# Where the sums for T4 and the low parts of T3 are made: in the last blocks of gMLP, or inside the first pair's products

## The chip, the cores and the metric

The kernel runs on one core of a Trainium2 chip. The metric is the device time of one execution in microseconds (us). Of the kernel before there are three timed runs and one profiled execution. The engines are named as the profile names them: PE is TensorE's matmuls, PEld its weight loads, DVE is VectorE, ACT is ScalarE, POOL is GpSimd, and SP is SyncE, which issues transfers.

## The reference, cut to what matters

One decoder layer over 1,024 tokens of width 1,024: a normalised input xn goes through one large projection `w_in`, its parts through three mixers (gMLP, RG-LRU, SSD), and the mixers' outputs are merged under gates and followed by an MLP.

```python
hn = rms_norm(h, norm_mix_g[l])
proj = jnp.einsum('bsd,de->bse', hn, w_in[l])
za, zb, zc, xbc, dt_raw, g_raw = jnp.split(proj, SPLIT_POINTS, axis=-1)
ya = gmlp_mixer(za, ...)
yb = rg_lru_mixer(zb, ...)
yc = ssd_mixer(zc, xbc, dt_raw, ...)
gates = jax.nn.sigmoid(g_raw.reshape(bsz, seq, N_BRANCHES, D_MODEL) + b_gate[l])
```

The change concerns only how the operands are made for the last part of `proj`: the gate columns `g_raw` (three branches), the SSD gate `zc` and part of the LRU gate.

## The kernel before, in words

**Split operands.** Every float32 operand of a matmul is kept as two fp32r tiles, a high part (a cast on ACT, line 132) and a low part (the difference, on DVE, line 133). `split` makes both. A product of two operands is three matmuls: high by high, high by low, low by high.

**Plain units.** The first part of `proj` is computed in units of 128 columns (`unit_in`, `one_unit`, lines 558 and 571): 48 matmuls of 128x512 at line 555 into a PSUM tile `ps` of 128x1,024, from a pool of two. The last eight units are those of gMLP, `gmlp_unit(g)` for g = 0 to 7. Each makes a gelu of its `ps` by four steps in a row, `gelu2` (lines 235 to 238: ACT, DVE, ACT, DVE; L238 is the last read of `ps`). Its `stages` then multiply the normalised v by the mixing weights (L836 on PE, L837 on DVE) and the gelu by that on POOL (L839), and POOL issues the store (L840).

**Steps.** Generators given to `later()` are advanced by `step()`, one piece at each call; `one_unit` calls it once after each unit. `x_forms`, the operand forms of X, is queued by the stages of g = 0. The order in these units is the scheduler's, by program order and readiness.

**Pairs.** The remaining columns are made in pairs of 2 x 128 columns with seven products instead of eight, each over half the depth: `seventh`, 12 matmuls of 128x512 at line 478. X is cut into quarters B11, B12, B21, B22, the weights into A11 to A22, and sums of quarters are used: T1, T2, T3, T4 of X, S1 to S4 of the weights. T3 is B22 - B12, T2 is B11 + T3, T1 is B22 - T2, and T4 is B21 - T2. The products of one pair are, in this order, p1 = A11 B11, p2 = A12 B21, p5 = S1 T1, p6 = S2 T2, p3 = S4 B22, p7 = S3 T3, and p4 = A22 T4. p1, p6, p7 and p4 accumulate in one PSUM bank of the pool `gps`, and between them the bank is read: after p1 by L981 and after p6 by L998 on ACT, after p7 by L1006 on DVE. p2's bank is read by L986 on DVE, the bank of p5 and p3 by L992 on ACT and L1002 on DVE. p4 stands behind p1 and p2 of the next pair. `gps` takes the banks in which `ps` lay.

**The order among the pairs** is that of the code, `tc.manual_schedule()` (line 1279): between the products stand the steps that prepare the next pair's weights (cast1; sums1, which is L502 and L503; sums2, L506 and L507; cast12; cast22) and this pair's S3 and S4 (cast34), and a `step()`, and each engine takes its instructions in that order. An instruction that waits holds all that is behind it on its engine.

**T3's low part and T4 in x_forms.** For each of two tiles kp the generator makes T3 unsplit (`third`, lines 871 to 873), T2 and its split, T1 and its split, and T4 (lines 883, 884 and a split into two tiles of the pool `act`, 15 buffers). At the very end, after the units, T3 is split over the tiles of B12, which nothing needs any more.

Of the kernel before, what the change touches and what calls it, by code (L numbers as in the profile page):

```python
# [8 lines left out]
F32 = mybir.dt.float32  # L9
# [27 lines left out]
def trunk_kernel(ctx: ExitStack, tc: tile.TileContext, x, norm_mix_g, w_in, b_gate, gmlp_ln_g, gmlp_ln_b,  # L37
# [30 lines left out]
    def nm(s):  # L68
        uid[0] += 1
        return f"{s}_{uid[0]}"  # L70

    def act(shape=(P, T), dt=F32):
        return pools[0].tile(list(shape), dt, tag="act", name=nm("a"))

    def half_(shape=(P, HF), dt=F32):
        return halfp.tile(list(shape), dt, tag="half", name=nm("h"))
# [51 lines left out]
    def split(dst_hi, dst_lo, src, eng=None, cast=None):  # L128
        if cast:
            cast.tensor_copy(out=dst_hi, in_=src)  # L130
        else:
            actv(dst_hi, src, AF.Copy)  # L132
        (eng or nc.vector).tensor_tensor(out=dst_lo, in0=src, in1=dst_hi.bitcast(F32), op=ALU.subtract)  # L133
# [62 lines left out]
    X = Pairs(lambda shape, dt_: xp.tile(list(shape), dt_, tag="xn", name=nm("xn")))  # L196
# [334 lines left out]
    queue, ready, pending = [], [], []  # L531
# [4 lines left out]
    def later(gen):  # L536
        pending.append(gen)

    def step():
        for g_ in list(pending):  # L540
            try:
                next(g_)
            except StopIteration:
                pending.remove(g_)
# [279 lines left out]
    def gmlp_unit(g):  # L824
        def stages(u2):
            if g == 0:
                later(x_forms())
            elif g == 5:
                later(first_pair())
            yield  # L830
            vg = v_of.pop(g)
            y = act()
            for half in range(2):
                ps = aux()
                for i in range(4):
                    mm(ps[:, i * P:(i + 1) * P], vg[:, half * 4 + i, :], wT[:, g, :], start=True, stop=True)  # L836
                stt(out=y[:, hsl(half)].rearrange("p (c t) -> p c t", t=P), in0=ps.rearrange("p (c t) -> p c t", t=P),  # L837
                    scalar=vh[:, LNG + g:LNG + g + 1], in1=bs[:, g, :].unsqueeze(1).to_broadcast([P, 4, P]), op0=ALU.mult, op1=ALU.add)
            nc.gpsimd.tensor_tensor(out=y, in0=y, in1=u2, op=ALU.mult)  # L839
            nc.gpsimd.dma_start(out=yd["a"][g], in_=y)  # L840

        def post(ps):
            u2 = act()
            gelu2(u2, ps, T)
            later(stages(u2))
            v_group(g + 1)

        unit_in(C_U + g * P, post)
# [2 lines left out]
    XF = {n: [[X.rhs(part, 4 * kh + kk, th) for kk in range(4)] for part in range(2)]  # L851
          for n, kh, th in (("B11", 0, 0), ("B21", 1, 0), ("B22", 1, 1), ("T3", 0, 1))}

    def x_forms():
        third = []
        for n in ("T1", "T2", "T4"):
            XF[n] = [[None] * 4, [None] * 4]
        for kp in range(2):
            def quarter(part, kh, th):
                return X.tile(part, th, 2 * kh + kp).bitcast(F32)  # L860

            def in_halves(name, t):
                for kk in range(2):
                    pr = half_((P, 4, P), F32R), half_((P, 4, P), F32R)
                    for part in range(2):
                        XF[name][part][2 * kp + kk] = pr[part]
                    split(pr[0], pr[1], t[:, kk])

            third.append(act((P, 2, 4, P)))
            t3, d, e = third[kp], act((P, 2, 4, P)), act((P, 2, 4, P))  # L870
            tt(out=t3, in0=quarter(0, 1, 1), in1=quarter(0, 0, 1), op=sub)
            tt(out=e, in0=quarter(1, 1, 1), in1=quarter(1, 0, 1), op=sub)
            tt(out=t3, in0=t3, in1=e, op=ALU.add)
            yield
            tt(out=d, in0=quarter(0, 0, 0), in1=t3, op=ALU.add)
            tt(out=d, in0=quarter(1, 0, 0), in1=d, op=ALU.add)
            in_halves("T2", d)
            yield
            tt(out=e, in0=quarter(0, 1, 1), in1=d, op=sub)
            tt(out=e, in0=quarter(1, 1, 1), in1=e, op=ALU.add)  # L880
            in_halves("T1", e)
            yield
            tt(out=d, in0=quarter(0, 1, 0), in1=d, op=sub)
            tt(out=d, in0=quarter(1, 1, 0), in1=d, op=ALU.add)
            pr = act((P, 2, 4, P), F32R), act((P, 2, 4, P), F32R)
            split(pr[0], pr[1], d)
            for part in range(2):
                for kk in range(2):
                    XF["T4"][part][2 * kp + kk] = pr[part][:, kk]
            yield  # L890
        assert not queue
        for kp in range(2):
            split(X.tile(0, 1, kp), X.tile(1, 1, kp), third[kp])

    actx_pool = []
    two = (P, 2, HF)
# [194 lines left out]
    def w_load(b, name, new, key=None):  # L1091
        L[b, key or name] = [new(two) for _ in range(2)]
        for h, t in enumerate(L[b, key or name]):
            nc.sync.dma_start(out=t, in_=w_view(b, name, h))
# [7 lines left out]
    def y_first(b, new):  # L1102
        R[b, "first"] = [new(two, F32R) for _ in range(2)]
        for h, t in enumerate(R[b, "first"]):
            nc.sync.dma_start(out=t.bitcast(F32), in_=y_view(b, "B21", h))
# [10 lines left out]
    def sums_load(b):  # L1116
        w_load(b, "A21", w4, "S")
        for h in range(2):
            add_into(L[b, "S"][h], w_view(b, "A22", h))
# [10 lines left out]
    def make(b, i, s):  # L1130

        side, h = (s // 2) ^ (i == 3), s % 2
        new = op_new(b, i, side)
        pr = OP.setdefault((b, i), ([], []))[side]
        if side == 0:
            src = L[b, ("A12", "A11", "S", "A12", "S", "A21", "A22")[i]][h]
            hi, lo = new(two, F32R), new(two, F32R)
            split(hi, lo, src)
            if i == 2:
                actv(src, src, AF.Copy, scale=-1.0)  # L1140
                add_into(src, L[b, "A11"][h])
                for k in range(2 * h):
                    add_into(L[b, "A12"][k], L[b, "S"][k])
            elif i == 4:
                t = L[b, "A21"][h]
                tt(out=t, in0=L[b, "A11"][h], in1=t, op=sub)
        elif i == 0:
            lo = R[b, "first"][h]
            hi = new(two, F32R)
            split(hi, lo, lo.bitcast(F32))  # L1150
        else:
            hi, lo = new(two, F32R), new(two, F32R)
            split(hi, lo, R[b, ("", "B11", "B11", "B22", "B11", "B12", "B21")[i]][h])
            r = lambda name: R[b, name][h]
            if i == 1:
                tt(out=r("B11"), in0=r("B12"), in1=r("B11"), op=sub)
            elif i == 3:
                tt(out=r("B11"), in0=r("B11"), in1=r("B22"), op=sub)
                tt(out=r("B12"), in0=r("B22"), in1=r("B12"), op=sub)
            elif i == 4:  # L1160
                tt(out=r("B21"), in0=r("B21"), in1=r("B11"), op=ALU.add)
        pr.append((hi, lo))
# [113 lines left out]
    gx = ExitStack()  # L1276
    actx_pool.append(gx.enter_context(tc.tile_pool(name="actx", bufs=4, reuse_waits="tile")))
    z, prev = cur.pop(), None
    with tc.manual_schedule():
        z.w.cast22()  # L1280
        while z:
            nxt = Pair(*pairs.pop(0)) if pairs else None
            z.p1()
            z.w.cast34()
            step()
            z.p2()
            if prev:
                step()
                prev.p4()
            if nxt:  # L1290
                nxt.w.cast1()
            else:
                w_load(0, "A12", r4)
                y_first(0, act)
                w_load(0, "A11", w4)
            step()
            z.p5()
            if nxt:
                nxt.w.sums1()
            else:  # L1300
                make(0, 0, 2)
            step()
            z.p6()
            if nxt:
                nxt.w.sums2()
                nxt.w.cast12()
            else:
                sums_load(0)
                make(0, 0, 3)
            step()  # L1310
            z.p3()
            if nxt:
                nxt.w.cast22()
            else:
                make(0, 0, 0)
            step()
            z.p7()
            if not nxt:
                make(0, 0, 1)
            step()  # L1320
            prev, z = z, nxt
# [532 lines left out]
```

## Time and profile before

| | |
|---|---|
| timed runs | 1976.08 us median of 3 (1975.45 to 1978.53) |
| profiled execution | 1979.05 us, span of the instructions 1977.3 us |
| granted TensorE clock, mean over the span | 0.986 |
| busy: PE, DVE, ACT, POOL | 1914.5, 1409.4, 1015.5, 256.9 us |
| the last gMLP products to p4 of the first pair | 600 to 648 us from the span's start |

Busy times are sums over instructions. A row of a timeline gives the start in us from the span's start, the duration, the engine, the line, the operation, the tiles out<-in and the number of instructions taken together; in brackets stands the idle time of that engine before it, and which instruction ended that. DVE and ACT begin an instruction a little before the one in front ends, so what an instruction takes in a queue is read from one start to the next.

### The profile page before, as it was taken

The page shows a single profiled execution, that of the slowest core. Times are in us where ns is not written, and L with a number is a line of the kernel's source. Part 1 is how long each engine was busy: PE and PEld are TensorE (multiplying, and loading weights), DVE is VectorE, ACT ScalarE, POOL GpSimd, SP SyncE. Part 2 cuts the span into 40 slices and gives each one's busy share as a digit, 9 for nine tenths or more (in the row PEclk, how much of TensorE's full clock was granted, in tenths as well). Part 3 has the DMA queues.
Part 4 walks back from the last instruction along what each step waited for, and adds up shares of the span by engine and source line. Part 5 has one row for each costly group of instructions (what it writes and reads, how often), then busy time and mean ns, then how long its engine had stood idle before and what let it go on. Part 6 is the DMA issues. An engine that isn't in the chain of part 4 may idle for free.

```text
span 1977.3 us, 23724 instructions
## 1 busy us (share of the span) xinstructions
PE 1914.5 (97%) x8928; PEld 1592.9 (81%) x8928; DVE 1409.4 (71%) x2018; ACT 1015.5 (51%) x1471; POOL 256.9 (13%) x358
## 2 busy tenths in 40 slices
PE   8999999999999999999999999998999999999996
PEld 7998878787887787878778888776788887888885
DVE  5485868686768676767767888347666657788787
ACT  6425858586633545454554544167555555243243
POOL 4111121112233010101010110000211110000000
PEclk8999999999999999999999999999999999999998
DMA  4246574666664252535298987321544458554632
GB/s 158 60 142 138 119 146 112 141 129 138 154 161 128 83 173 87 169 91 165 98 296 277 253 230 191 138 104 60 193 136 165 134 181 303 171 162 117 190 115 88
DMA packets 211015, 301.25 MB, mean 152 GB/s; under 512 B 13028, under 2 KB 125876, under 8 KB 210900
## 3 DMA queue, kind: packets, MB, share of 16 engines
q1 hardware_dynamic: 167348, 158.54, 26.4%
q0 software_dynamic: 34544, 119.69, 22.7%
q10 hardware_dynamic: 9008, 21.51, 3.1%
q8 instruction: 70, 1.15, 0.3%
q14 instruction: 45, 0.37, 0.1%
HBM read 195.75 MB, written 74.58 MB: 137 GB/s over the span
## 4 chain that ended last, share of the span: by engine, by line
PE 68%; DVE 11%; issue 7%; ACT 7%; DMA 6%; POOL 1%; ACTq 0%; POOLq 0%; DVEq 0%; SPq 0%
PE aux L478 39%; PE ps L555 10%; PE gps L478 8%; PE aux L257 5%; PE aux L1376 2%; DMA a<-acs_d 2%; DVE a L578 1%; DMA raw<-in_w_in_dram 1%; DMA c<-yc_d 1%; ACT a L1425 1%; DMA wl<-raw 1%; PE aux L789 1%; DVE a L133 1%; DVE rsq_q L111 1%; DVE wt L133 1%
## 5 line engine op out<-in xcount | busy, mean ns | idle before, releaser
L555 PE MATMUL ps<-xn,wh 128*128 128x512 f32 x1088 | 294.8, 392 | 0.0
L478 PE MATMUL aux<-b,b 128*128 128x512 f32 x1152 | 264.4, 389 | 0.9 <-DVE b L133 0.9
L478 PEld LDWEIGHTS aux<-b,b 128*128 128x128 f32 x1152 | 216.1, 188 | 46.9 <-DVE b L133 1.7
L555 PEld LDWEIGHTS ps<-xn,wh 128*128 128x128 f32 x1088 | 202.9, 188 | 42.1 <-issue 0.7
L478 PE MATMUL aux<-a,b 128*128 128x512 f32 x960 | 219.4, 389 | 0.0
L478 PEld LDWEIGHTS aux<-a,b 128*128 128x128 f32 x960 | 180.2, 188 | 37.4
L555 PE MATMUL ps<-xn,wl 128*128 128x512 f32 x544 | 167.6, 389 | 0.0
L478 PE MATMUL gps<-xn,wt 128*128 128x512 f32 x684 | 160.2, 392 | 2.1 <-DVE a L238 2.1
L478 PE MATMUL aux<-b,wt 128*128 128x512 f32 x672 | 156.9, 389 | 0.0
L478 PEld LDWEIGHTS gps<-xn,wt 128*128 128x128 f32 x684 | 129.4, 189 | 29.4 <-issue 2.5
L478 PEld LDWEIGHTS aux<-b,wt 128*128 128x128 f32 x672 | 126.2, 188 | 26.2
L132 ACT ACTIVATE b<-wt 128x1024 fp32r<-128x1024 f32 x88 | 90.9, 1054 | 85.5 <-DMA wt<-u_d 55.3
L133 DVE TENSOR_TENSOR wt<-a,wt 128x1024 fp32r<-128x1024 f32 x66 | 80.9, 1226 | 66.9 <-ACT wt L132 66.9
L555 PEld LDWEIGHTS ps<-xn,wl 128*128 128x128 f32 x544 | 102.1, 188 | 21.5
L133 DVE TENSOR_TENSOR b<-wt,b 128x1024 fp32r<-128x1024 f32 x88 | 107.2, 1219 | 15.7 <-ACT b L132 15.7
L1606 DVE TENSOR_TENSOR a<-aux,a 128x512 f32<-128x512 f32 x112 | 77.0, 689 | 50.4 <-PE aux L478 50.4
L133 DVE TENSOR_TENSOR a<-a,a 128x1024 fp32r<-128x1024 f32 (+1 forms) x68 | 66.6, 986 | 41.2 <-ACT a L132 41.1
L133 DVE TENSOR_TENSOR wt<-rt,wt 128x1024 fp32r<-128x1024 f32 x35 | 42.9, 1225 | 57.1 <-ACT wt L132 57.0
L478 PE MATMUL aux<-a,wt 128*128 128x512 f32 x336 | 80.3, 396 | 3.3 <-ACT a L1483 3.3
L132 ACT ACTIVATE a<-a 128x1024 fp32r<-128x1024 f32 (+1 forms) x68 | 55.9, 838 | 53.4 <-DVE a L1558 45.1
L478 PEld LDWEIGHTS aux<-a,wt 128*128 128x128 f32 x336 | 64.1, 191 | 17.6 <-ACT a L1483 4.2
L132 ACT ACTIVATE wt<-a 128x1024 fp32r<-128x1024 f32 x66 | 69.6, 1054 | 8.8 <-DVE a L506 8.3
(349 smaller groups left out, 3533.3 us busy)
## 6 DMA issues: line engine op xcount, KB each, us to landing
wt<-u_d SPq DMA_DIRECT2D x54, 512.0 KB
u_d<-a POOLq DMA_DIRECT2D x48, 512.0 KB, 5.4
raw<-in_w_in_dram SPq DMA_DIRECT2D x34, 512.0 KB
wl<-raw POOLq DMA_DIRECT2D x34, 512.0 KB, 5.3
g_d<-a POOLq DMA_DIRECT2D x24, 512.0 KB, 3.4
a<-g_d ACTq DMA_DIRECT2D x24, 512.0 KB
rt<-in_w_in_dram SPq DMA_DIRECT2D x19, 512.0 KB
a<-in_w_in_dram SPq DMA_DIRECT2D x19, 512.0 KB
```

Of the source, the lines that this page charges most:

```text
L111: stt(out=q, in0=r, scalar=nh, in1=r, op0=ALU.mult, op1=ALU.mult)
L132: actv(dst_hi, src, AF.Copy)
L133: (eng or nc.vector).tensor_tensor(out=dst_lo, in0=src, in1=dst_hi.bitcast(F32), op=ALU.subtract)
L257: mm(ps[:, :nt], X.tok(a, k, c), wk[k][w], start=(k == 0 and i == 0), stop=(k == KD - 1 and i == 2))
L478: mm(ps, lhs[l][kk], rhs[r][kk], start=(new and n == 0), stop=(n == 11), skip_group_check=not new)
L555: mm(ps[:, hsl(h)], w[wi][:, k, :], a.rhs(ai, k, h), start=(n == 0), stop=(n == 3 * KD - 1))
L578: stt(out=dst[:, j:], in0=ps[:, :T - j], scalar=taps[3 - j], in1=dst[:, j:], op0=ALU.mult, op1=ALU.add)
L789: mm(ps, w[wi][:, q * P:(q + 1) * P], S["xs"][half][ai], start=(n == 0), stop=(n == 2))
L1376: mm(ps, M.tok(a, k, c), wo[nb][k][w], start=(k == 0 and a + w == 0), stop=(k == KD - 1 and a == 1))
L1425: actv(Nf[th, k // 2][:, k % 2, (c % 4) * P:(c % 4 + 1) * P], ps[:, i * P:(i + 1) * P], AF.Identity, scale=g2c[:, KD + k:KD + k + 1])
L1606: tt(out=h, in0=ps, in1=h, op=ALU.add)
```

## The change

`third` becomes a list of the kernel function, beside a new one, `second`, which keeps each T2 unsplit. `x_forms` ends with T1. Its two pieces for T4 and the final splits of T3 move into a new generator, `x_last`, which is queued before the first pair's products. The first `step()` inside the pair (after p1 and cast34) makes the split of T3's first tile, the second (after the next pair's cast1) that of the second tile, the third (after p5 and sums1) T4's first tile, and the fourth (after p6, sums2 and cast12) T4's second tile. `x_forms` no longer has a step of its own between the first tile's T1 and the second tile's T3, so the second tile's T3, T2 and T1 come one unit earlier.

```diff
--- before.py
+++ after.py
@@ -851,8 +851,9 @@
     XF = {n: [[X.rhs(part, 4 * kh + kk, th) for kk in range(4)] for part in range(2)]
           for n, kh, th in (("B11", 0, 0), ("B21", 1, 0), ("B22", 1, 1), ("T3", 0, 1))}
 
+    third, second = [], []
+
     def x_forms():
-        third = []
         for n in ("T1", "T2", "T4"):
             XF[n] = [[None] * 4, [None] * 4]
         for kp in range(2):
@@ -880,6 +881,19 @@
             tt(out=e, in0=quarter(1, 1, 1), in1=e, op=ALU.add)
             in_halves("T1", e)
             yield
+            second.append(d)
+
+
+    def x_last():
+        assert not queue
+        for kp in range(2):
+            split(X.tile(0, 1, kp), X.tile(1, 1, kp), third[kp])
+            yield
+        for kp in range(2):
+            def quarter(part, kh, th):
+                return X.tile(part, th, 2 * kh + kp).bitcast(F32)
+
+            d = second[kp]
             tt(out=d, in0=quarter(0, 1, 0), in1=d, op=sub)
             tt(out=d, in0=quarter(1, 1, 0), in1=d, op=ALU.add)
             pr = act((P, 2, 4, P), F32R), act((P, 2, 4, P), F32R)
@@ -888,9 +902,6 @@
                 for kk in range(2):
                     XF["T4"][part][2 * kp + kk] = pr[part][:, kk]
             yield
-        assert not queue
-        for kp in range(2):
-            split(X.tile(0, 1, kp), X.tile(1, 1, kp), third[kp])
 
     actx_pool = []
     two = (P, 2, HF)
@@ -1276,6 +1287,7 @@
     gx = ExitStack()
     actx_pool.append(gx.enter_context(tc.tile_pool(name="actx", bufs=4, reuse_waits="tile")))
     z, prev = cur.pop(), None
+    later(x_last())
     with tc.manual_schedule():
         z.w.cast22()
         while z:
```

The instructions are the same ones, as many on each engine; PE, POOL and SP keep their order. Line numbers behind the change are larger: L883 and L884 (T4's sums) become L897 and L898, L981 becomes L992, L992 becomes L1003, L998 becomes L1009, L986 becomes L997, L1006 becomes L1017, L915 becomes L926.

First place: DVE, around the last unit's gelu, before. `a_768` is T4 in the making (L883, L884) and T2 before that, `a_769` is T1, `h` are halves of a low part, `xn_79` is T3's first low part, and `a_788` and `a_787` belong to the last gelu.

```order
L133 TENSOR_TENSOR h_778_5314<-a_768_5234,h_777_5313 128x512
L880 TENSOR_TENSOR a_769_5235<-xn_85_561,a_769_5235 128x1024
L133 TENSOR_TENSOR h_780_5318<-a_768_5234,h_779_5317 128x512
L133 TENSOR_TENSOR xn_79_543<-a_717_4900,xn_77_537 128x1024
L133 TENSOR_TENSOR h_790_5398<-a_769_5235,h_789_5397 128x512
L883 TENSOR_TENSOR a_768_5234<-xn_41_239,a_768_5234 128x1024
L236 SCALAR_TENSOR_TENSOR a_788_5390<-a_788_5390,ps_786_5340 128x1024
L133 TENSOR_TENSOR h_792_5402<-a_769_5235,h_791_5401 128x512
L884 TENSOR_TENSOR a_768_5234<-xn_43_246,a_768_5234 128x1024
L238 SCALAR_TENSOR_TENSOR a_787_5389<-a_788_5390,ps_786_5340 128x1024
```

Now, the same place, from the gelu of the unit before (`a_777`) to the first weight sum of the next step.

```order
L133 TENSOR_TENSOR h_771_5240<-a_756_5149,h_770_5239 128x512
L133 TENSOR_TENSOR h_780_5318<-a_757_5150,h_779_5317 128x512
L133 TENSOR_TENSOR h_782_5322<-a_757_5150,h_781_5321 128x512
L236 SCALAR_TENSOR_TENSOR a_777_5308<-a_777_5308,ps_775_5258 128x1024
L238 SCALAR_TENSOR_TENSOR a_776_5307<-a_777_5308,ps_775_5258 128x1024
L837 SCALAR_TENSOR_TENSOR a_783_5325<-aux_784_5326,vh_810,bs_95 128x512
L837 SCALAR_TENSOR_TENSOR a_783_5325<-aux_785_5332,vh_810,bs_95 128x512
L236 SCALAR_TENSOR_TENSOR a_790_5394<-a_790_5394,ps_788_5344 128x1024
L238 SCALAR_TENSOR_TENSOR a_789_5393<-a_790_5394,ps_788_5344 128x1024
L502 TENSOR_TENSOR a_793_5403<-a_787_5341 128x512
```

The two sums of T4 and T3's low part are gone from in front of the last L238, and T1's low parts stand ahead of the gelu of the unit before.

Second place: ACT, from the last gelu to the copies of the first pair, before. `a_800` is the cast of T4's second tile, `wt` are casts of weights, `a_811` and `a_818` the outputs of the first pair, `gps_810` the bank of p1, p6 and p7.

```order
L237 ACTIVATE a_788_5390<-a_788_5390 128x1024
L132 ACTIVATE a_800_5432<-a_768_5234 128x1024
L132 ACTIVATE wt_802_5436<-a_795_5409 128x1024
L132 ACTIVATE a_807_5470<-a_785_5337 128x512
L981 ACTIVATE a_811_5490<-gps_810_5477 128x512
L132 ACTIVATE wt_812_5492<-a_796_5410 128x1024
L132 ACTIVATE wt_815_5510<-rt_808_5473 128x1024
L992 ACTIVATE a_818_5527<-aux_817_5514 128x512
L915 ACTIVATE a_811_5490<-a_811_5490,vh_810 128x512
L998 ACTIVATE a_818_5527<-gps_810_5477 128x512
```

Now `gps_806` is that bank, `a_717` and `a_755` are T3, `a_718` is T4's first tile, `a_814` and `a_807` the outputs of the pair.

```order
L237 ACTIVATE a_790_5394<-a_790_5394 128x1024
L132 ACTIVATE wt_798_5424<-a_793_5403 128x1024
L132 ACTIVATE a_803_5454<-a_787_5341 128x512
L992 ACTIVATE a_807_5474<-gps_806_5461 128x512
L132 ACTIVATE wt_808_5476<-a_794_5404 128x1024
L132 ACTIVATE xn_77_537<-a_717_4900 128x1024
L132 ACTIVATE wt_811_5496<-rt_804_5457 128x1024
L132 ACTIVATE xn_78_540<-a_755_5148 128x1024
L1003 ACTIVATE a_814_5515<-aux_813_5502 128x512
L926 ACTIVATE a_807_5474<-a_807_5474,vh_810 128x512
L132 ACTIVATE a_817_5524<-a_718_4901 128x1024
L1009 ACTIVATE a_814_5515<-gps_806_5461 128x512
```

The cast of T4's first tile (`a_817`) now stands ahead of the copy of p6 (L1009), and the two casts of T3 ahead of the copy of p5 (L1003).

Third place: DVE, from the low part of S3 and S4 on, before. `wt_813` is that low part, `gps_814` is p2, `rt_808` and `a_809` are the second pair's weights.

```order
L133 TENSOR_TENSOR wt_813_5493<-a_796_5410,wt_812_5492 128x1024
L986 TENSOR_TENSOR a_811_5490<-gps_814_5496,a_811_5490 128x512
L133 TENSOR_TENSOR wt_816_5511<-rt_808_5473,wt_815_5510 128x1024
L502 TENSOR_TENSOR a_819_5530<-a_809_5474 128x512
L503 TENSOR_TENSOR a_820_5531<-rt_808_5473,a_809_5474 128x512
L506 TENSOR_TENSOR a_819_5530<-a_819_5530,rt_808_5473 128x512
L507 TENSOR_TENSOR a_820_5531<-rt_808_5473,a_819_5530 128x512
L133 TENSOR_TENSOR wt_822_5550<-a_819_5530,wt_821_5549 128x1024
L1002 TENSOR_TENSOR a_818_5527<-aux_817_5514,a_818_5527 128x512
```

Now `wt_809` is that low part, and `rt_804` and `a_805` are the second pair's weights.

```order
L133 TENSOR_TENSOR wt_809_5477<-a_794_5404,wt_808_5476 128x1024
L133 TENSOR_TENSOR xn_79_543<-a_717_4900,xn_77_537 128x1024
L997 TENSOR_TENSOR a_807_5474<-gps_810_5482,a_807_5474 128x512
L133 TENSOR_TENSOR wt_812_5497<-rt_804_5457,wt_811_5496 128x1024
L133 TENSOR_TENSOR xn_80_546<-a_755_5148,xn_78_540 128x1024
L502 TENSOR_TENSOR a_815_5518<-a_805_5458 128x512
L503 TENSOR_TENSOR a_816_5519<-rt_804_5457,a_805_5458 128x512
L897 TENSOR_TENSOR a_718_4901<-xn_40_236,a_718_4901 128x1024
L898 TENSOR_TENSOR a_718_4901<-xn_42_243,a_718_4901 128x1024
L133 TENSOR_TENSOR a_818_5525<-a_718_4901,a_817_5524 128x1024
```

The two low parts of T3 (`xn_79`, `xn_80`) and T4's sums and low part now stand between the second pair's weights, and L506 comes behind T4's first tile.

## Rows read from the trace of the kernel before

**Rows 1.** The page's busy time, share of the span and instructions of each engine.

```profile
PE 1914.5 (97%) x8928; PEld 1592.9 (81%) x8928; DVE 1409.4 (71%) x2018; ACT 1015.5 (51%) x1471; POOL 256.9 (13%) x358
```

**Rows 2.** Timeline of PE from the unit before the last to p3 of the first pair: start, duration, line, tiles, count, and in brackets the idle time before it and its releaser. `gps<-xn,wt` are p1 and p2, `aux<-h,wt` p5, `gps<-h,wt` p6, `aux<-xn,wt` p3.

```profile
600.58 1.95 PE L836 MATMUL aux<-wT,a 128*128 128x128 f32 x16
...
613.26 3.73 PE L836 MATMUL aux<-wT,a 128*128 128x128 f32 x32
616.75 2.98 PE L478 MATMUL gps<-xn,wt 128*128 128x512 f32 x12
621.83 4.57 PE L478 MATMUL gps<-xn,wt 128*128 128x512 f32 x12 [2.10 <-DVE a L238]
626.24 0.62 PE L478 MATMUL aux<-h,wt 128*128 128x512 f32 x2
627.73 2.59 PE L478 MATMUL aux<-h,wt 128*128 128x512 f32 x10 [0.87 <-DVE wt L133]
630.63 3.02 PE L478 MATMUL gps<-h,wt 128*128 128x512 f32 x12 [0.30 <-ACT a L981]
633.48 0.61 PE L478 MATMUL aux<-xn,wt 128*128 128x512 f32 x2
635.02 2.56 PE L478 MATMUL aux<-xn,wt 128*128 128x512 f32 x10 [0.93 <-DVE wt L133]
```

**Rows 3.** Timeline of PE behind that: 36 matmuls of p7 and of the next pair's p1 and p2, then p4.

```profile
637.42 8.32 PE L478 MATMUL gps<-xn,wt 128*128 128x512 f32 x36
645.58 2.88 PE L478 MATMUL gps<-a,a 128*128 128x512 f32 x12
```

**Rows 4.** PE in stretches of 2 us: busy time (matmuls), granted clock, share and rate of the transfers.

```profile
622.00:624.00 2.00, 2.00 (x7) 0.64 0.49 117
624.00:626.00 2.00, 2.00 (x6) 0.51 0.53 152
626.00:628.00 2.00, 1.13 (x5) 1.00 0.89 248
```

**Rows 5.** Timeline of DVE from the gelu of the unit before the last to the low part of S3 and S4 (`wt<-a,wt` at 633.76; that of S1 and S2 is at 626.46).

```profile
604.32 1.22 DVE L238 SCALAR_TENSOR_TENSOR a<-a,ps 128x1024 f32<-128x1024 f32 x1 [1.20 <-ACT a L237]
...
616.47 1.21 DVE L883 TENSOR_TENSOR a<-xn,a 128x1024 f32<-128x1024 f32 x1
617.60 1.21 DVE L236 SCALAR_TENSOR_TENSOR a<-a,ps 128x1024 f32<-128x1024 f32 x1
618.73 0.68 DVE L133 TENSOR_TENSOR h<-a,h 128x512 fp32r<-128x512 f32 x1
619.34 1.22 DVE L884 TENSOR_TENSOR a<-xn,a 128x1024 f32<-128x1024 f32 x1
620.47 1.21 DVE L238 SCALAR_TENSOR_TENSOR a<-a,ps 128x1024 f32<-128x1024 f32 x1
...
626.46 1.22 DVE L133 TENSOR_TENSOR wt<-a,wt 128x1024 fp32r<-128x1024 f32 x1
627.60 1.40 DVE L837 SCALAR_TENSOR_TENSOR a<-aux,vh,bs 128x512 f32<-128x512 f32 x2
628.92 2.10 DVE L133 TENSOR_TENSOR xn<-a,xn 128x1024 fp32r<-128x1024 f32 x1
630.95 2.89 DVE L133 TENSOR_TENSOR a<-a,a 128x512 fp32r<-128x512 f32 x1
633.76 1.21 DVE L133 TENSOR_TENSOR wt<-a,wt 128x1024 fp32r<-128x1024 f32 x1
```

**Rows 6.** Timeline of ACT over the same stretch: the first step of the last two gelus (L235), a cast-sized step (L237), the copies of p1 (L981) and of p6 (L998).

```profile
600.84 1.02 ACT L235 ACTIVATE a<-ps 128x1024 f32<-128x1024 f32 x1 [8.65 <-PE ps L555]
...
614.78 1.00 ACT L235 ACTIVATE a<-ps 128x1024 f32<-128x1024 f32 x1
...
618.85 1.06 ACT L237 ACTIVATE a<-a 128x1024 f32<-128x1024 f32 x1 [2.55 <-DVE a L236]
...
629.98 0.60 ACT L981 ACTIVATE a<-gps 128x512 f32<-128x512 f32 x1 [4.88 <-POOL a L839]
...
636.24 0.59 ACT L998 ACTIVATE a<-gps 128x512 f32<-128x512 f32 x1
```

**Rows 7.** Timeline of POOL: the last two products of gMLP (L839) and the issue of the store between them.

```profile
625.50 4.44 POOL L839 TENSOR_TENSOR a<-a,a 128x1024 f32<-128x1024 f32 x1 [12.11 <-DVE a L837]
630.24 0.58 POOL L840 DMA_DIRECT2D ya_d<-a  x1 [0.30 <-POOL a L839]
630.85 2.44 POOL L839 TENSOR_TENSOR a<-a,a 128x1024 f32<-128x1024 f32 x1
```

**Rows 8.** All engines from 535 to 600: busy time and number of instructions of PE, PEld, DVE, ACT and POOL, then the granted clock and the transfers.

```profile
535.00:600.00 65.00, 65.00 (x342) 55.37 (x343) 44.19 (x43) 19.76 (x22) 25.71 (x20) 1.00 0.57 146
```

**Rows 9.** SP's queue: when it issued the loads of the third and the fourth pair's second weight tile.

```profile
631.05 0.37 SPq L488 DMA_DIRECT2D a<-in_w_in_dram  x1
...
646.25 0.37 SPq L488 DMA_DIRECT2D a<-in_w_in_dram  x1
```

**Rows 10.** Timeline of DVE: the first instructions that read those two weight tiles.

```profile
651.32 0.69 DVE L502 TENSOR_TENSOR a<-a 128x512 f32<-128x512 f32 x1
...
670.26 0.69 DVE L502 TENSOR_TENSOR a<-a 128x512 f32<-128x512 f32 x1
```

## The prediction

> **What bounds the kernel now.** I read the page's busy times first, then the timeline of TensorE (PE) across the end of gMLP, then VectorE (DVE), ScalarE (ACT) and GpSimd (POOL) over the same stretch. PE is busy for 97% of the span [rows 1], so the end moves only if PE's idle time, or its clock, changes. Nearly all that this change can touch is in one place: the first pair of the gate projections. Its seven products of 12 matmuls run in the order p1, p2, p5, p6, p3, p7, then p1 and p2 of the next pair, then p4. The reader is to see in [rows 2] that p1 starts at 616.75 without a wait and that p2, p5, p6 and p3 all wait, and in [rows 3] that p7 starts at 637.42 and p4 at 645.58, with nothing between them: 36 matmuls in 8.16 us, so 2.72 us a product. p1 to p3 are five products, 13.60 us, and took 637.42 - 616.75 = 20.67 us: 7.07 us are lost. That is what there is to win. The largest piece is p2: it idles 2.10 us for the last gelu's L238, and then runs its 12 matmuls in 4.41 us (621.83 to 626.24), since the granted clock stood at 0.64 and 0.51 between 622 and 626 [rows 4], at or near the lower of its two levels, 1.2 of 2.4 GHz.
>
> **Step 1: the last gelu.** DVE is full there [rows 5]: L883 and L884 (T4's sums) stand ahead of L238, and ACT reaches the last L235 only at 614.78 behind casts of T1 [rows 6]. In the changed order neither is there: T1's casts are one unit earlier. One unit before, L235 started at 600.84 [rows 6] and L238 3.48 us later, at 604.32 [rows 5], with nothing in between. The last product ends 12.68 us after that one (distance of the L836 blocks behind them, 600.58 to 613.26 [rows 2]), so L235 starts at about 613.52 and L238 at 617.00, done at 618.2 instead of 621.68. p1 ends at 616.75 + 2.72 = 619.47: p2 no longer waits, PE has no idle time here, and I count full clock. p2 ends at 622.2 (before 626.24).
>
> **Step 2: p5, p6, p3.** From L238 to the low part of S1 (626.46) were 5.99 us, 1.13 of them T4's low part. Without it the low part is issued at 621.86 and done at 623.08; p5's third matmul starts then (before 627.73). p5 ends at 625.4. p6 waited for L981, and that for POOL's L839 [rows 2, 6]; the copy's tile now has another former owner, which is done, so p6 follows: 628.1. p3 needs the low part of S3 and S4. Ahead of it are two L837 (1.32 us, 627.60 to 628.92) and A22's low part, which stands still until POOL's product ends. Before, that product (begun 625.50) ended at 629.94, 2.34 us after the L837s began [rows 5, 7]; now at 622.99 + 2.34 = 625.33. Low part of A22 0.55 behind it (633.84 against 633.29 before), 625.9; low part of S3 and S4 at 627.0. p3 runs from 628.1 to 630.8: 6.6 us earlier than before.
>
> **Step 3: what is late next.** p7 accumulates into the bank of p6, so it waits for ACT's copy of p6 (L998 before, done at 636.83 [rows 6], which cost p7 nothing; L1009 now). In the new ACT order a cast of T4 stands ahead of that copy, and it waits for DVE's second sum of T4 (L898). On DVE ahead of L898's end stand, from 626.93 on: T3's low part, L997, the next pair's low part, T3's second low part, L502, L503, L897, L898. With 1.13 us for 1,024 elements (616.47 to 617.60), 0.60 for 512 (618.73 to 619.34), 1.21 for the last and 0.1 for its own operand, that is 7.6 us: 634.6 if nothing comes between. POOL's eighth product does. It is issued 0.91 us after the seventh ends (629.94 to 630.85 [rows 7]), at 626.24, and beside it a DVE instruction with both inputs in SBUF is held: the 512-element one took 2.89 instead of 0.68, the 1,024-element one 2.10 instead of 1.21 [rows 5].
>
> Whether DVE is held is the unknown. From below, nothing: one such instruction passed a POOL product already issued without loss (626.46, 1.22 us [rows 5], POOL since 625.50 [rows 7]). From above, the whole product, 2.44 us [rows 7]. The Trainium skill (GPSIMD Engine Reference, 1. Specifications) says that GpSimd shares its SBUF interfaces with VectorE and contends with DVE instructions that have two SBUF inputs; most of those listed have. By that rule one of them is held, which is the forecast; if the rule did nothing here, it would be rival (a).
>
> I take it that one is held, as two of the three in [rows 5] that met a POOL product were. If POOL comes in under L997, which reads PSUM: from 628.06 to 630.40, the next low part done 1.08 later at 631.5, L898 at 636.2. If it comes in one instruction earlier: L898 at 636.8. Then ACT's cast 1.06 [rows 6] and the copy 0.59: p7 starts at 637.9 or 638.5, against 637.42. So the 6.6 us won are all given back at p7, where PE idles 7.1 to 7.7 us.
>
> **Step 4: p4.** After an idle of 2.10 us the clock fell [rows 4]; after 7 us I count p7 as slow as p2 was, 4.41 us. PE alone would reach p4 at 637.9 + 4.41 + 2 x 2.72 = 647.75 (or 648.35). DVE is a little later still. p4 needs L1017, DVE's read of p7, which now stands behind all of T4's second half. From L898's end: cast 1.1, T4 low part 1.26, L506 and L507 1.3 (ACT's cast of the next S1 after L506 sets the next low part, done 5.3 after L898), two sums 2.35, cast 1.1, low part 1.25, then L1013, a low part and L1017, 1.8: some 11.8 us with the hand-overs. L1017 is done at 648.0 (or 648.6), and p4 starts then, against 645.58: +2.5 or +3.1, middle **+2.8 us**.
>
> **What costs nothing.** Nothing is removed or added: T4 has the same four sums, two casts and two low parts, and PE, POOL and SP have the same order. Earlier, DVE loses T4's first half beside units in which PE never waited (65.00 us busy of 65.00 from 535 to 600 [rows 8]). T1's casts now hold the gelu of the unit before by 2.3 us; its bank is not needed again. On SP the third pair's weight load (631.05 before [rows 9]) now waits for the store of the last gMLP block: POOL's end 630.4, 0.3 and 0.6 to issue, some 5 us to land, so about 636; its reader was at 651.32 [rows 10], 15 us later. The next one (646.25 before) now waits for p4's end, 650.8; its reader was at 670.26. After p4 all follows PE as before, so 2.8 us stay to the end.
>
> The profiled execution took 1979.05 us (span 1977.3), 2.97 above the median of the runs, 1976.08. The sum is 1979.05 + 2.8 = 1981.9 in the profile's terms, and **1978.9** in those of the median.
>
> **Rivals.** (a) POOL's product does not hold DVE: L898 at 634.6, p7 at 636.3, L1017 at 646.4, so +0.9: 1977.0. For it the row at 626.46, against it those at 628.92 and 630.95 [rows 5]. Here belongs, too, that the change does nothing at all that shows: p7's release comes from another instruction at nearly the same moment. (b) Slower: the clock stays low past p7. It decides once more than p7 runs slowly, for then PE and no longer DVE is late at p4: each further product costs 1.69 us (4.41 - 2.72). With p1 slow too p4 starts at 637.9 + 2 x 4.41 + 2.72 = 649.4, with p2 as well at 651.1: +3.8 to +5.5, 1980.8. For it: the idle is three times the 2.10 us that came before [rows 4]; against it: there the clock stood at 1.00 again from 626 on, and the products behind p2 ran at it. (c) Faster: the waits of p2 to p3 are gone and none replaces them, -6.6 us, 1969.5. For it: the early waits do vanish. Against it: both orders; p4 would need T4's second half by 639, and DVE, full without a gap, has it at 646.
>
> **The numbers.** Forecast 0.62 (its own range 1977.7 to 1980.2), (a) 0.20, (b) 0.13, (c) 0.05. About 0.2%, 3.95 us, is what a measurement of this kernel can tell from no change: 1972.1 to 1980.0. Slower takes (b) and a small tail of the forecast, 0.19; faster is (c), 0.05; the rest, 0.76, within. For 8 in 10 the range runs from within (a) to the middle of (b), 1976.2 to 1980.9.
>
> **What would show it.** Right: no wait of p2 on L238 and clock 1.00 under it; p3 done near 631; one PE wait of some 7 us at p7 on ACT L1009, then a low clock; p4 waiting for L1017 near 648. Wrong: p7 starting near 631, or p4 before 645.6 (then (c)); DVE rows without one of 2 us or more after 626 (then (a)); p1 and p2 of the second pair longer than 2.72 us (then (b)).

## The result and the profile after

The changed kernel takes 1979.68 us (median of 15 runs, 1978.03 to 1982.4) against 1976.08 of the kernel before. The ratio is 1.0018 (95% interval 1.0010 to 1.0025), so it is 2 to 5 us slower. The forecast was 1978.9, +2.8 us, its own range 1977.7 to 1980.2. The ratio lies inside the 0.2% that I took for the bound of no change, but its interval doesn't reach 1.

The profiled execution took 1979.34 us, its span 1977.6, which is only 0.3 longer than that of before. The difference is in where each trace reached the end of gMLP: its last L836 block starts at 609.53 here and at 613.26 before [rows 2]. The 3.73 us between them are not the change's doing, as second traces of both kernels show below. So all that follows is measured from the start of that block, called the block from here on, and the mark behind the stretch is p6 of the second pair, two products behind p4.

First the page's busy times of the changed kernel, then the timeline of TensorE from the last L836 block on (start, duration, line, tiles, count, in brackets the idle time before and its releaser). `gps<-xn,wt` x24 are p1 and p2, then come p5, p6, p3, and x36 are p7 and the next pair's p1 and p2; `gps<-a,a` is p4.

```profile
PE 1912.7 (97%) x8928; PEld 1590.7 (80%) x8928; DVE 1410.4 (71%) x2018; ACT 1014.9 (51%) x1471; POOL 255.2 (13%) x358
```

```profile
609.53 3.73 PE L836 MATMUL aux<-wT,a 128*128 128x128 f32 x32
613.01 5.70 PE L478 MATMUL gps<-xn,wt 128*128 128x512 f32 x24
618.55 3.32 PE L478 MATMUL aux<-h,wt 128*128 128x512 f32 x12
621.71 2.88 PE L478 MATMUL gps<-h,wt 128*128 128x512 f32 x12
624.43 0.61 PE L478 MATMUL aux<-xn,wt 128*128 128x512 f32 x2
625.98 2.57 PE L478 MATMUL aux<-xn,wt 128*128 128x512 f32 x10 [0.93 <-DVE wt L133]
635.22 10.43 PE L478 MATMUL gps<-xn,wt 128*128 128x512 f32 x36 [6.67 <-ACT a L1009]
645.61 3.02 PE L478 MATMUL gps<-a,a 128*128 128x512 f32 x12
...
651.18 2.88 PE L478 MATMUL gps<-h,wt 128*128 128x512 f32 x12
```

The waits of p2, p5 and p6 [rows 2] are gone. p3 ends 19.0 us behind the start of the L836 block, where before it took 24.2 (637.42 - 613.26). Then comes one wait of 6.67 us, for ScalarE's copy of p6. Behind it 36 matmuls take 10.39 us instead of 8.16 [rows 3]. p4 starts 36.08 us behind the block, against 32.32 before.

p6 of the second pair, the last row, starts 41.65 us behind the block. In the kernel before this was 37.76 (651.02 - 613.26), by this row:

```profile
651.02 2.88 PE L478 MATMUL gps<-h,wt 128*128 128x512 f32 x12
```

That is 3.89 us more. The busy times hardly differ from [rows 1], and from that mark to the end of the span the two traces take as long, 1326.3 us before and 1326.4 now. So the loss is in this stretch.

Next, what stands in front of that copy: DVE, ScalarE and GpSimd in the same trace.

```profile
622.00 3.93 DVE L133 TENSOR_TENSOR wt<-a,wt 128x1024 fp32r<-128x1024 f32 x1
...
632.30 1.23 DVE L898 TENSOR_TENSOR a<-xn,a 128x1024 f32<-128x1024 f32 x1
...
644.87 0.69 DVE L1017 TENSOR_TENSOR a<-gps,a 128x512 f32<-128x512 f32 x1
```

```profile
633.62 1.06 ACT L132 ACTIVATE a<-a 128x1024 fp32r<-128x1024 f32 x1 [5.20 <-DVE a L898]
634.59 0.58 ACT L1009 ACTIVATE a<-gps 128x512 f32<-128x512 f32 x1
```

```profile
618.28 3.24 POOL L839 TENSOR_TENSOR a<-a,a 128x1024 f32<-128x1024 f32 x1 [9.47 <-DVE a L837]
...
622.42 2.41 POOL L839 TENSOR_TENSOR a<-a,a 128x1024 f32<-128x1024 f32 x1
```

L898, T4's second sum, ends at 633.53. ScalarE has been idle for 5.20 us by then: its cast waits for L898, and the copy L1009 stands behind the cast. The reader sees GpSimd hold up DVE (the low part of S3 and S4 takes 3.93 us beside a product), DVE hold up ScalarE, and ScalarE hold up TensorE. L1017 ends at 645.56 and p4 starts at 645.61. The 36 matmuls in front of it end just then too, and the profile shows no wait of p4. So which of the two set p4's start can't be told.

### The profile page after: what moved, and what is told of

Read it like the earlier page. It is cut to its first block, busy times and chain, and to the rows that moved or that the text cites. A ratio compares the mean times of both kernels' runs of the same rounds, so it can differ in the third digit from the quotient of the medians.

```text
span 1977.6 us, 23717 instructions
## 1 busy us (share of the span) xinstructions
PE 1912.7 (97%) x8928; PEld 1590.7 (80%) x8928; DVE 1410.4 (71%) x2018; ACT 1014.9 (51%) x1471; POOL 255.2 (13%) x358
## 4 chain that ended last, share of the span: by engine, by line
PE 68%; DVE 11%; issue 8%; ACT 7%; DMA 6%; POOL 1%; ACTq 0%; POOLq 0%; DVEq 0%; SPq 0%
PE aux L478 39%; PE ps L555 10%; PE gps L478 9%; PE aux L257 4%; PE aux L1388 2%; DMA a<-acs_d 1%; DVE a L578 1%; DMA raw<-in_w_in_dram 1%; DMA c<-yc_d 1%; ACT a L1437 1%; DMA wl<-raw 1%; DVE rsq_q L111 1%; ACT a L132 1%; DVE a L133 1%; DMA a<-g_d 1%
## 5 line engine op out<-in xcount | busy, mean ns | idle before, releaser
L133 DVE TENSOR_TENSOR a<-a,a 128x512 fp32r<-128x512 f32 (+1 forms) x68 | 65.3, 967 | 43.5 <-ACT a L132 43.4
L132 ACT ACTIVATE a<-a 128x512 fp32r<-128x512 f32 (+1 forms) x68 | 55.8, 838 | 61.1 <-DVE a L1570 45.1
```

## The experiments

One table first, from the ten traces. All times are in us from the start of the last L836 block; "p6 of pair 2" is where that product starts, and "against before" is the difference at that mark. The ratios are against the kernel before on the same chip: it took 1974.46 us (28 runs) beside e1 to e4, and 1974.62 (27 runs) beside e5, e6 and the changed kernel's second ratio; its first ratio is against the 1976.08 above. The changed kernel has 15 and 11 runs, e1 has 6, and e2 to e6 have 11 each. The expected times start from 1976.08, so they are compared by ratio.

| kernel | T3's low parts | T4 | p4 | p6 of pair 2 | against before | ratio (95% interval) |
|---|---|---|---|---|---|---|
| before, two traces | end of units | end of units | 32.32, 32.33 | 37.76, 37.77 | | |
| changed, two traces | pair | pair | 36.08, 36.06 | 41.65, 41.64 | +3.88 | 1.0018 (1.0010 to 1.0025); 1.0023 (1.0014 to 1.0032) |
| e1 | pair | pair, cast behind the copy | 34.89 | 43.00 | +5.24 | 1.0033 (1.0022 to 1.0045) |
| e2 | pair | units, one earlier | 27.89 | 33.34 | -4.42 | 0.9984 (0.9976 to 0.9993) |
| e3 | units, one earlier | pair | 33.87 | 39.44 | +1.68 | 1.0019 (1.0010 to 1.0028) |
| e4 | pair | pair, one POOL product out | 33.97 | 39.41 | +1.65 | 1.0015 (1.0006 to 1.0024) |
| e5 | units, one earlier | units, one earlier | 26.95 | 32.40 | -5.36 | 0.9978 (0.9970 to 0.9987) |
| e6 | pair | end of units | 32.07 | 37.51 | -0.25 | 1.0002 (0.9993 to 1.0011) |

The seven ratios from the later chips (all but the changed kernel's first) lie 0.6 to 2.1 us above the traces' differences. Only that of e3, the farthest, has the trace's difference outside its interval, but all seven lie on the same side, and why stays open. Behind p6 of pair 2 the ten traces take between 1325.9 and 1328.4 us to the end, e3's the longest. So a difference of a us or two between kernels is read in the stretch, and there it rests on one trace of each experiment.

**Both kernels again.** Nothing is edited.

> The kernel before once more, for a second trace. If the 3.7 us by which its first trace reached the last L836 block later than the changed kernel's (613.26 against 609.53) is chance of that execution and not the change, the second trace reaches it near 609.5 and takes 37.8 us from there to p6 of the second pair; if it is the change, near 613.

> The changed kernel once more, for its trace and its time on the chip of these runs: 1.0018 of the kernel before, and 41.65 us from the last L836 block to p6 of the second pair. If the time between them is set by the order and the clock, the second trace agrees within 1 us.

The second trace of the kernel before reaches the block at 607.98, that of the changed kernel at 608.32, so the late 613.26 does not come from the change. From the block on each agrees with its first trace within 0.01 us (37.77 and 37.76, 41.64 and 41.65). On this chip the changed kernel took 1979.59 us against 1974.62. TensorE in the second trace of the kernel before, and its granted clock (the last three columns: clock, share and rate of the transfers):

```profile
607.98 3.73 PE L836 MATMUL aux<-wT,a 128*128 128x128 f32 x32
611.46 2.98 PE L478 MATMUL gps<-xn,wt 128*128 128x512 f32 x12
616.54 2.99 PE L478 MATMUL gps<-xn,wt 128*128 128x512 f32 x12 [2.10 <-DVE a L238]
619.37 0.72 PE L478 MATMUL aux<-h,wt 128*128 128x512 f32 x2
622.44 2.56 PE L478 MATMUL aux<-h,wt 128*128 128x512 f32 x10 [2.35 <-DVE wt L133]
```

```profile
616.00:618.00 2.00, 1.46 (x6) 1.24 (x7) 2.00 (x4) 0.41 (x1) 0.00 (x0) 1.00 0.14 36
618.00:620.00 2.00, 2.00 (x9) 1.24 (x7) 2.00 (x4) 1.58 (x2) 0.00 (x0) 1.00 0.80 226
```

p2 idles the same 2.10 us, but the clock stays at 1.00 and p2 takes 2.83 us instead of 4.41 [rows 2, 4]. Nothing is won by it. p5 now waits 2.35 us for its low part instead of 0.87, and its third matmul starts 14.46 us behind the block, against 14.47 in the first trace. DVE sets that moment. p2's low clock was covered.

**e1: the copy ahead of the cast.** Against the changed kernel:

```diff
+            if kp == 0:
+                yield
             split(pr[0], pr[1], d)
...
                     XF["T4"][part][2 * kp + kk] = pr[part][:, kk]
-            yield
```

> The changed kernel, with only the cast and low part of T4's first tile moved behind p6's copy (its two sums stay where they are), so that ScalarE's copy no longer waits for DVE's sums. Theory A (T4 itself, 7 us of DVE work with its hand-overs, is too late for p4 wherever p7 waits): p7 follows p3 at about 629 instead of 635.2 (times as in the trace of the changed kernel), but p4 now waits for DVE's read of p7, which DVE reaches at about 644, so PE is idle some 7 us in front of p4, the clock falls there instead, and the time stays within -1.6 to +0.6 us of the changed kernel: 1978.1 to 1980.3 us. Rival B (the place of the copy in ScalarE's order is the whole loss): the idle time at p7 goes and no other comes, -6.7 us and no low clock: 1971 to 1973 us.

```profile
628.74 8.46 PE L478 MATMUL gps<-xn,wt 128*128 128x512 f32 x36 [0.41 <-ACT a L1010]
644.20 5.46 PE L478 MATMUL gps<-a,a 128*128 128x512 f32 x12 [7.01 <-DVE a L1018]
649.46 3.02 PE L478 MATMUL aux<-h,wt 128*128 128x512 f32 x12
```

p7 follows p3, and 7.01 us of idle time now stand in front of p4: rival B falls. p4 starts 1.2 us earlier than in the changed kernel, about as expected, and still the stretch is 1.35 us longer. The slow matmuls now lie behind the wait for L1018 (p4 takes 5.26 us to the start of the next product, not 2.72), where nothing covers them. In the changed kernel p7 ran slowly while DVE was still busy with what p4 waits for. Theory A's place of the new wait is right and its size too small: I had up to +0.6 us against the changed kernel, and it is +1.35, because the slow matmuls cost 2.7 us (8.11 from p4 to p6 where 5.44 is full speed), not 2.2, and p4 won 1.2, not 1.6. The ratio, 1.0033, agrees (+6.5 us, interval 4.3 to 8.9).

**e2: T4 back in the units.** In `x_forms`, and without T4 in `x_last`:

```diff
             in_halves("T1", e)
-            yield
-            second.append(d)
+            tt(out=d, in0=quarter(0, 1, 0), in1=d, op=sub)
+            tt(out=d, in0=quarter(1, 1, 0), in1=d, op=ALU.add)
+            pr = act((P, 2, 4, P), F32R), act((P, 2, 4, P), F32R)
+            split(pr[0], pr[1], d)
...
+            yield
```

> The changed kernel with T4 made right behind T1 in the gMLP units again (one unit earlier than in the kernel before), and only T3's low parts made beside the first pair. Theory A: nothing waits from p3 to p4 any more; p7 follows p3, and p4 starts 27.2 us behind the last gMLP products' start (32.3 before, 36.1 in the changed kernel): -8.9 us against the changed kernel if the last gelu stays where it is, 1970.8 us; DVE is fuller in the unit before the last by about 5 us, so p2 may wait up to 3 us: 1970.8 to 1974. Rival C (the loss comes from T3's low parts beside the pair, or from X's forms one unit earlier): the time stays at the changed kernel's, 1979.7 us.

```profile
608.87 3.73 PE L836 MATMUL aux<-wT,a 128*128 128x128 f32 x32
...
621.48 3.02 PE L478 MATMUL gps<-h,wt 128*128 128x512 f32 x12 [0.32 <-ACT a L985]
625.75 3.01 PE L478 MATMUL aux<-xn,wt 128*128 128x512 f32 x12 [1.25 <-ACT a L996]
628.61 8.32 PE L478 MATMUL gps<-xn,wt 128*128 128x512 f32 x36
636.76 2.88 PE L478 MATMUL gps<-a,a 128*128 128x512 f32 x12
...
642.21 2.88 PE L478 MATMUL gps<-h,wt 128*128 128x512 f32 x12
```

p6 waits 0.32 us for the copy of p1 (L985 here) and p3 1.25 us for the copy of p5 (L996, behind T3's two casts). From p3's start to p4 nothing waits. 8.31 us of the stretch are gone against the changed kernel, and the kernel is faster than before: 1971.45 us, by the ratio 1.4 to 4.7 us less. p2 does not wait. Rival C falls as the whole cause.

**e3: T4 late alone.** T3's two splits go to the end of `x_forms`, behind a `while queue: yield`, and the two steps in `x_last` are left empty.

> The changed kernel with T3's two casts and low parts put back between the units and the pair, ahead of the last gelu's second half, and T4 left where the change puts it. Theory A: L238 comes 2 us later and DVE has 2.3 us less in front of T4's sums, so p7 still waits about as long for p6's copy and p4 starts as late: within -1 to +1 us of the changed kernel, 1978.7 to 1980.7 us. Rival C (T3's part is what makes it late): -2.3 us or more, 1977.4 us or less.

```profile
603.00 4.55 DVE L133 TENSOR_TENSOR xn<-a,xn 128x1024 fp32r<-128x1024 f32 x2
...
608.45 1.22 DVE L236 SCALAR_TENSOR_TENSOR a<-a,ps 128x1024 f32<-128x1024 f32 x1 [0.91 <-ACT a L235]
```

```profile
607.15 3.73 PE L836 MATMUL aux<-wT,a 128*128 128x128 f32 x32
...
630.55 10.03 PE L478 MATMUL gps<-xn,wt 128*128 128x512 f32 x36 [4.40 <-ACT a L1011]
641.02 3.02 PE L478 MATMUL gps<-a,a 128*128 128x512 f32 x12 [0.44 <-DVE a L1019]
...
646.59 2.88 PE L478 MATMUL gps<-h,wt 128*128 128x512 f32 x12
```

A miss for theory A's number: the low parts are done in a gap in front of the last gelu, and DVE still waits 0.91 us for L235, so L238 is not late. The 2.3 us less on DVE come out in full: p7 waits 4.40 instead of 6.67 us, and the stretch is 2.21 us shorter than in the changed kernel. By the trace T3's part costs something too, as rival C had it, but with T4 alone the kernel is still behind the one before. The timed runs don't show the 2.2 us: the ratio is 1.0019, that of the changed kernel 1.0018 and 1.0023. It stands for +2.0 to +5.5 us, a little above the +1.68 of the trace. What is missing there stays open.

**e4: the last product on GpSimd left out.** The last unit's mixed values are stored without the gelu's factor.

```diff
-            nc.gpsimd.tensor_tensor(out=y, in0=y, in1=u2, op=ALU.mult)
+            if g < 7:
+                nc.gpsimd.tensor_tensor(out=y, in0=y, in1=u2, op=ALU.mult)
```

> The changed kernel without GpSimd's product of the last gMLP unit (mixed values times gelu; that part of the output is left out). In the trace of the changed kernel the low part of S3 and S4 takes 3.93 us instead of 1.21, beside that product. Theory A, step 3 (GpSimd's product holds DVE): that row is 1.2 us, p3's wait of 0.93 us goes, L898, p7 and p4 come 2.7 us earlier: 1977.0 us. Rival D (the row is long for another reason, such as its wait for ScalarE's cast): the row stays near 3.9 us and the time at 1979.7 us.

```profile
621.03 1.21 DVE L133 TENSOR_TENSOR wt<-a,wt 128x1024 fp32r<-128x1024 f32 x1
```

```profile
623.47 2.88 PE L478 MATMUL aux<-xn,wt 128*128 128x512 f32 x12
631.52 11.17 PE L478 MATMUL gps<-xn,wt 128*128 128x512 f32 x36 [5.17 <-ACT a L1010]
642.53 2.88 PE L478 MATMUL gps<-a,a 128*128 128x512 f32 x12
```

The low part of S3 and S4 takes 1.21 us instead of 3.93, p3 doesn't wait, and p7 starts 22.96 us behind the block instead of 25.69, the 2.7 us expected. Rival D falls. p4 comes only 2.1 us earlier, because the 36 matmuls took 11.01 us: this time the low clock lasted longer. DVE's read of p7 (L1018 here) was done at 641.79, 0.74 us before p4 starts, so here TensorE's slow matmuls set p4, and not DVE. The timed ratio, 1.0015, cannot tell 2.2 us less from the changed kernel's 1.0018 and 1.0023; the verdict rests on the rows.

**e5: everything in the units, one earlier.** Against the kernel before, one step goes:

```diff
             in_halves("T1", e)
-            yield
```

(and the `assert` in front of T3's splits becomes `while queue: yield`).

> The kernel before with one edit: x_forms loses its step between T1 and T4, so T4 is made right behind T1, and all forms and T3's low parts come one unit earlier; nothing is made beside the first pair. From the start of the last gMLP products (the last L836 block) to p6 of the second pair it took 37.76 us in the kernel before, 41.65 in the changed one and 33.34 with T4 alone back in the units. Theory A (what costs is T4 and T3 on DVE and ScalarE beside the pair): T3's two casts no longer stand ahead of the copy of p5, so p3's wait of 1.25 us shrinks to what the low part of S3 and S4 asks: about 32.2, another 1.2 us less, -5.6 us against the kernel before, 1970.5 us. Rival E (DVE becomes too full ahead of the last gelu and p2 waits for L238 again): 34 to 37, 1972 to 1975.5 us.

```profile
606.56 3.73 PE L836 MATMUL aux<-wT,a 128*128 128x128 f32 x32
...
622.96 2.56 PE L478 MATMUL aux<-xn,wt 128*128 128x512 f32 x10 [0.93 <-DVE wt L133]
625.36 8.32 PE L478 MATMUL gps<-xn,wt 128*128 128x512 f32 x36
633.51 2.88 PE L478 MATMUL gps<-a,a 128*128 128x512 f32 x12
...
638.96 2.88 PE L478 MATMUL gps<-h,wt 128*128 128x512 f32 x12
```

32.40 us, as expected (32.2): the only wait from p1 to p4 that the timeline names is p3's 0.93, for the low part of S3 and S4, which takes 3.92 us here too. It beats both kernels: 1969.91 us, 2.6 to 5.9 us less than the kernel before by the ratio. Rival E falls: DVE's two low parts are done by 606.7, and L236 at 607.81 still waits for ScalarE.

**e6: T3 late alone, T4 where it was.** The T4 lines go back into `x_forms` with their own step.

> The changed kernel with T4 made exactly where the kernel before makes it (a step of its own behind T1, so the forms are a unit later again), and T3's low parts left beside the first pair. Theory A: L238 stands behind T4's sums again, only T3's first low part (1.13 us) is gone from in front of it: p2 waits about 1 us instead of 2.10, p7 does not wait for p6's copy. From the last L836 block to p6 of the second pair 35 to 37.8 us (37.76 before): 1973.3 to 1976.1 us. Rival F (the early gain comes from T3's move and not from T4's): p2 does not wait, 33.5 us or less, 1971.8 us or less.

```profile
618.03 3.00 PE L478 MATMUL gps<-xn,wt 128*128 128x512 f32 x12 [1.76 <-DVE a L238]
620.87 0.70 PE L478 MATMUL aux<-h,wt 128*128 128x512 f32 x2
623.93 2.54 PE L478 MATMUL aux<-h,wt 128*128 128x512 f32 x10 [2.36 <-DVE wt L133]
```

p2 waits 1.76 us for L238, where I expected about 1, p5 waits 2.36, as in the second trace of the kernel before (2.35), and next to nothing is won (0.25 us in the stretch, 1.0002). Rival F falls.

**What these add up to.** e5, e2, e3 and the changed kernel differ only in which of the two jobs stands beside the pair:

| p6 of pair 2 | T4 in the units | T4 in the pair |
|---|---|---|
| T3's low parts in the units | 32.40 (e5) | 39.44 (e3) |
| T3's low parts in the pair | 33.34 (e2) | 41.65 (changed) |

The step that `x_forms` lost is worth -5.37 us (37.77 to 32.40). T3 beside the pair gives back 0.94, T4 7.04, and both together 1.27 more: -5.37 + 0.94 + 7.04 + 1.27 = +3.88. The 1.27 fits that DVE then does both in a row in front of L898, but it rests on single traces, and the timed ratios of e3 and the changed kernel don't show it. T3's 0.94 isn't all T3's work either: 0.32 of it is p6's wait in e2 for L985, which waits for GpSimd's L839 as L981 did in the kernel before [rows 6], and e5 has no such wait.

The change contains its gain and its loss as two edits, and the gain needs neither of the moves. Whether moving T4 away with the step kept would win as much in front of L238 was not run.

## Why the prediction was right, and where it was off

The forecast case is the one that came. Its steps in us from the start of the L836 block, forecast times less 613.26:

| | forecast | trace |
|---|---|---|
| p5, p6, p3 start | 8.9, 12.1, 14.8 | 9.0, 12.2, 14.9 |
| p3 ends | 17.5 | 19.0 |
| L898 done | 22.9 or 23.5 | 24.0 |
| p7 starts | 24.6 or 25.2 | 25.7 |
| p4 starts | 34.8 or 35.4 | 36.1 |

- Steps 1 and 2 hold: no wait for L238, full clock under p2 (1.00 throughout), p6 without a wait. One reading of the kernel before in front of them was wrong. I called p2's low clock a large piece of the 7.07 us that are lost; the second trace has none and loses the same. The sum did not rest on it, because step 2 took p5 from DVE's order.
- Step 3 holds in its mechanism: the copy behind T4's cast, the cast behind L898, and GpSimd's product in front of both. The instruction that was held is another one. I had the low part of S3 and S4 slip through and one of T3's low parts, or the next pair's, held; the trace holds S3 and S4's low part itself, for 2.7 us (3.93 against 1.21 in e4). That delays p3 as well. The sum still nearly fits because both stand in front of L898, so one product's hold goes into it either way. I had counted the hold as 1.6 or 2.2 us there, and it was 2.7, so L898 came 0.5 to 1.1 us later than forecast.
- Step 4 adds the rest. From the end of L898 to that of L1017 it took 12.0 us, where I had 11.8, and the 36 matmuls took 10.39 us, where I had 9.85 (4.41 + 2 x 2.72). Both came due within 0.1 us, so that p4 waits for DVE and not for the slow matmuls, as I had it, is not shown: the profile shows no such wait here. It does in e1 and e3, and in e4 it was the matmuls. The forecast of +2.5 to +3.1 us at p4 became +3.76 there, and +3.6 in the timed medians.
- "What costs nothing" held, with one size off: the third pair's weight load waited for the store, as forecast, but left SP at 628.13, 18.6 us behind the block (17.8 before [rows 9]). I had it 22.7 behind, at 636. The store had landed earlier than I gave it.
- Rival (a), GpSimd without effect: false, since the row that takes 3.93 us takes 1.21 in e4. Rival (b): the clock is low for about the first ten matmuls (an estimate: 10.39 - 8.16 = 2.23 us, and a matmul at half the clock takes 0.23 us longer), no further than p7. In e4, with 2.85 us, it is low just past p7, and p4 is late by TensorE, as (b) had it. Rival (c), no new wait: false for this change, but e2 and e5 show what it would have been worth, -4.4 and -5.4 us; I had -6.6.

The clock over p7 in the changed kernel (the column behind GpSimd's busy time):

```profile
632.00:634.00 2.00, 0.00 (x0) 0.00 (x0) 1.49 (x2) 0.38 (x1) 0.00 (x0) 0.66 1.01 373
634.00:636.00 2.00, 0.78 (x2) 0.69 (x3) 1.22 (x2) 1.16 (x2) 0.00 (x0) 0.50 0.08 31
636.00:638.00 2.00, 2.00 (x7) 1.52 (x6) 1.57 (x4) 1.06 (x1) 0.00 (x0) 0.50 0.00 0
638.00:640.00 2.00, 2.00 (x7) 1.62 (x6) 2.00 (x2) 0.00 (x0) 0.00 (x0) 0.64 0.71 185
640.00:642.00 2.00, 2.00 (x10) 1.64 (x9) 1.32 (x2) 0.56 (x1) 0.00 (x0) 1.00 0.27 82
```

It is at 0.50, the lower level of 1.2 GHz, from before p7's start until shortly before 640.

## What to carry to other kernels

Work that is moved out of a stage because it stands in front of something has to be placed by what is behind it in its new queues, on each engine that it uses: here ScalarE's cast brought DVE's wait in front of a copy that TensorE needed. If the wait is taken away alone (e1), the next deadline of the same work shows it again. A change that makes several edits is best split in a table of runs with each edit alone; the one that won was a deleted `yield`.

## What the runs showed that was not expected

- DVE and GpSimd hold each other, and which one waits differs. In the changed kernel DVE's low part took 3.93 us beside GpSimd's product of 2.41, which takes 2.39 with DVE idle (at 605.54); without the product the low part took 1.21. In e5 it is the other way: DVE's two low parts run at full speed, and the product, issued 0.17 us behind the first, takes 4.40 us.

```profile
604.30 2.35 DVE L133 TENSOR_TENSOR xn<-a,xn 128x1024 fp32r<-128x1024 f32 x2
```

```profile
604.47 4.40 POOL L839 TENSOR_TENSOR a<-a,a 128x1024 f32<-128x1024 f32 x1 [8.29 <-DVE a L837]
```

  So the row at 626.46 in [rows 5], which passed a product, stands beside a product of 4.44 us [rows 7]: there it may have been GpSimd that waited. The Trainium skill (Trainium Architecture — The Big Picture, the second of its three mental-model corrections) calls the port pair that the two share an exclusive lock and not a split of bandwidth. The rows agree: one waits out the other instead of both running slower, and e4 gives the price, 2.7 us. Which row begins first doesn't decide who waits: DVE's begins 0.42 us ahead of the product in the changed kernel (622.00 and 622.42) and is held, and 0.17 us ahead in e5 and is not. No run here shows what does.

- How long the clock stays low doesn't follow from the idle time before it. After 2.10 us of idle it fell in one trace of the kernel before and not in the other. p7 and what follows took 1.9 us longer than at full clock after an idle of 4.40 us (e3, 10.03 against 8.16), 2.9 us longer after 5.17 (e4, 11.01), 2.2 us longer after 6.67 (10.39), and p4 in e1 2.5 longer after 7.01. The Trainium skill (TensorE: Matmul & The Clock Gate, Part 1) says that the number of slow matmuls at a kernel's start varies from run to run for the same kernel. Here, in the middle of one, the two traces of the kernel before differ in that way, and the two of the changed kernel do not (10.39 us in both). A term for it has to be a range, and what it costs depends on the other engines: nothing in the kernel before, where DVE was late in the same stretch, and all of it in e1.
